# A gated trunk layer in float32 pairs: the order of the last two gate cells, the first loads, and the sums of squares

## The chip, the cores and the metric

One Trainium2 chip, one NeuronCore in use. The metric is the device time of one execution of the whole program in microseconds (us), the median of several runs. A profile of one execution gives the times of single instructions. The engines are called PE (TensorE, the matrix engine), DVE (VectorE), ACT (ScalarE), POOL (GpSimd) and SP (SyncE, which here only issues transfers).

## What is computed

One decoder layer (sequence 1024, width 1024) and a final RMSNorm. Shortened:

```python
h = rms_norm(x, norm_mix_g)
q, k, v, z_a, gk_low, cb, cc, xc, z_c, g_a, g_c = split(h @ w_in)
gk = log_sigmoid(gk_low @ w_gk2 + b_gk) / 16
o = rms_norm(gla_chunked(q, k, v, gk), gla_norm_g)        # linear attention, 4 heads, chunks of 64
y_a = (o * silu(z_a)) @ w_branch_a
y_c = ((cb * causal_dwconv(cc * xc, conv_w)) * silu(z_c)) @ w_branch_c
merged = sigmoid(g_a + b_ga) * y_a + sigmoid(g_c + b_gc) * y_c
x = x + merged @ w_out
ple_gate = sigmoid(rms_norm(x, norm_ple_g) @ w_ple_gate)
x = x + ple_gate * (p @ w_ple_proj)                        # p: (1024, 256)
return rms_norm(x, norm_final_g)
```

## The kernel before

**Products.** Every large product is made from pairs: a float32 tile is split into a rounded part `hi` (a cast on ACT) and a rest `lo = src - hi` (a subtraction on DVE), and `mm3` issues three matrix instructions for one 128x512 product: hi times hi, hi times lo, lo times hi. Large products go by a seven-product scheme for a two by two split (products 0 to 6 in place of eight). A `Cell` holds one such scheme for 256 rows or columns of the result. Product k of a cell takes twelve matrix instructions (four K-tiles times three). The running sums are in three PSUM banks X, Y and V: products 0 and 3 end in X, which is quarter (0,0); Y starts as a copy of product 0 and takes 2, 4 and 6; V takes 1 and 5. Two intermediate values are kept in SBUF: `c12` (tag u2, Y after product 2) and `c22` (tag s5, V after product 1). Quarter (0,1) is V after product 5 plus c12, quarter (1,1) is Y after product 4 plus c22, quarter (1,0) is Y after product 6. `cons(i, j, src)` consumes a finished quarter. `run_groups` lists the products of the cells; in a pair the two cells alternate product by product, in the order `PAIR` (0, 1, 2, 3, 5, 4, 6). Operands are loaded and split up to seven products ahead.

**Stages.** At the start the projection `pe` = p times w_ple_proj is computed in blocks of 128 rows (`pe_blocks`) and stored to DRAM, while x is loaded. Ten filler products (`warm`) on a cleared tile (`zero`) run before it. `scale_h` forms the mean squares of x for one half of the sequence: four squares on ACT (scaled by 1/32), added on DVE into a tile of two K-tiles, then summed over the partitions by one-column products with a vector of ones (`ms`), four blocks of 128 tokens times two K-tiles, each in full float32. From the result come r (a power on POOL), its transposes `rt` and the scaled `hq`. Then come the gates, v, the conv branch, attention woven between the gate cells, the two branch projections, the output projection (`out0` to `out3`), and last the gate cells `gt0` to `gt3`, 256 rows each, with everything that closes the layer in their consumer.

**The closing.** For each quarter of a gate cell: a sigmoid on ACT with the row scale `rg`, its product with `pe` and the addition to x on DVE, and the square of the new x on ACT with an accumulated row sum. When both halves of a row are there, `rf` = (mean square + eps) to the power -1/2 on POOL, then the multiplication with rf and the gain `gf`, and a store. For some rows (`late_cons`, `piece`) the first half is multiplied by gf in advance. The very last product (cell 3, product 6) is made in two halves of 256 columns (`last_product`), the second into another bank, Z.

**Order.** The program is recorded first (`Flow.note`), with a cost for each instruction and a latency behind it. `set_dues` works back from the end to a due time for each, and `put_in_order` steps through time, taking for the engine that is free first the ready instruction with the earliest due time; on PE the products of the cells keep their written order (`side = False`), and others (sums, transposes, attention) fall between. `hurry` moves a due time up. The result is a fixed order for each engine, SP's queue of transfers included, and each engine runs it strictly in that order. All compute instructions are recorded through one helper, so the profile shows them all at one line (L491) and they are told apart by their tiles.

Of the kernel before, what the change touches and what calls it, by code (L numbers as in the profile page):

```python
# [246 lines left out]
class Flow:  # L247
# [12 lines left out]
    def note(self, engine, op, call, args, kw):  # L260
# [15 lines left out]
        if engine == PE:  # L276
            o.cost, o.lat = n / 2400 + 0.0134, 0.22
            if op == "transpose" or args[1].dtype == F32:
                o.cost = 0.11
            elif args[1].shape[0] < P:  # L280
                o.cost = 0.42
# [10 lines left out]
        elif engine == POOL:  # L292
            o.cost = 0.1 + n * 0.001 if op == "memset" else 0.6
# [110 lines left out]
    def put_in_order(self):  # L404
# [28 lines left out]
        while len(order) < len(ops):  # L433
            best = None
            for e in range(5):
# [12 lines left out]
                best = (when, e, first[1] if pick is None else pick)  # L448
            assert best, "nothing can run"
# [49 lines left out]
START = 30.0  # L499


@with_exitstack
def kernel(
# [197 lines left out]

    ORDER, PAIR = tuple(range(7)), (0, 1, 2, 3, 5, 4, 6)

    class Cell:


        def __init__(self, name, side, src, res, cons, prods=ORDER, begin=None, s1=None, u2=None, s5=None, fresh=()):
# [3 lines left out]
            self.s1, self.seed, self.ready, self.halves = s1, None, lambda k: True, None  # L711
# [12 lines left out]
        def prep(self, k):  # L724
            if k not in self.ring:
                self.load(k)
                self.ring[k] = self.steps[k]()
# [35 lines left out]
        def run(self, k):  # L763
            if k == self.prods[0]:
                if self.begin:
                    self.begin()
                self.Y = None
# [5 lines left out]
            elif k == 1:  # L773
# [28 lines left out]
    def line_up(groups):  # L802
# [3 lines left out]
        return [(c, k) for g in groups for k in g[0].prods for c in g]  # L806

    def single(cs):
        return [[c] for c in cs]

# [175 lines left out]
    nc.vector.memset(f(zero), 0.0)  # L986
# [4 lines left out]
    for n in range(10):  # L991
        mm(warm[n % 6], zero[:, 0:P], zero, start=True, stop=True)
    nc.side = True

    with phase("prep0") as pool:
# [37 lines left out]
        def scale_h(i):  # L1033
# [30 lines left out]
        def pe_blocks(bs, c, by_kt=False):  # L1064
# [5 lines left out]
            todo = [(b, kt) for kt in range(2) for b in bs] if by_kt else [(b, kt) for b in bs for kt in range(2)]  # L1070
# [709 lines left out]
```

## Time and profile before

| | |
|---|---|
| time, median of 3 runs | 1102.06 us (1101.98 to 1102.79) |
| the profiled execution: its own time | 1102.23 us |
| its span, first to last instruction | 1100.4 us |
| PE busy | 1089.4 us, 99% of the span |
| DVE, ACT, POOL busy | 855.8, 598.2, 56.0 us |
| granted PE clock | 0.998 |

Rows of the timeline read: start in us, duration in us, engine, line, operation, output tile <- input tiles, shapes, count; in brackets the time that the engine stood idle before it, and what ended that. Matrix instructions overlap, so the distance between their starts tells more than their durations. The chain of waits follows the work that ended last back to the start. SPq is SP's queue of transfers: its rows tell when a transfer was issued, not when it landed.

### The profile page before, as it was taken

The page shows a single profiled execution, that of the slowest core. Times are in us where ns is not written, and L with a number is a line of the kernel's source. Part 1 is how long each engine was busy: PE and PEld are TensorE (multiplying, and loading weights), DVE is VectorE, ACT ScalarE, POOL GpSimd, SP SyncE. Part 2 cuts the span into 40 slices and gives each one's busy share as a digit, 9 for nine tenths or more (in the row PEclk, how much of TensorE's full clock was granted, in tenths as well). Part 3 has the DMA queues.
Part 4 walks back from the last instruction along what each step waited for, and adds up shares of the span by engine and source line. Part 5 has one row for each costly group of instructions (what it writes and reads, how often), then busy time and mean ns, then how long its engine had stood idle before and what let it go on. Part 6 is the DMA issues. An engine that isn't in the chain of part 4 may idle for free.

```text
span 1100.4 us, 15273 instructions
## 1 busy us (share of the span) xinstructions
PE 1089.4 (99%) x5050; PEld 908.3 (83%) x5050; DVE 855.8 (78%) x1386; ACT 598.2 (54%) x1107; POOL 56.0 (5%) x116
## 2 busy tenths in 40 slices
PE   9999999999999999999999999999999999999996
PEld 7888888788888888888888898888888888888885
DVE  6996477789878878748649587876999889868666
ACT  6775347866543554343333377766736445457554
POOL 0000000000000000000000022230000000002021
PEclk9999999999999999999999999999999999999999
DMA  9957463358867595222212699988595888889653
GB/s 317 327 184 246 131 210 109 117 172 252 255 221 268 177 313 180 88 66 66 87 58 65 220 307 345 323 267 293 207 308 176 301 260 291 293 311 320 238 201 114
DMA packets 152574, 238.94 MB, mean 217 GB/s; under 512 B 12976, under 2 KB 66480, under 8 KB 149424
## 3 DMA queue, kind: packets, MB, share of 16 engines
q1 hardware_dynamic: 152496, 237.98, 65.0%
q8 instruction: 39, 0.64, 0.2%
q14 instruction: 39, 0.32, 0.1%
HBM read 157.19 MB, written 80.74 MB: 216 GB/s over the span
## 4 chain that ended last, share of the span: by engine, by line
PE 96%; ACT 2%; DVE 2%; issue 0%; POOL 0%; DVEq 0%; ACTq 0%
PE vacc L491 7%; PE op L491 3%; PE pe L491 2%; PE X L491 2%; PE ga2Y L491 1%; PE ga3Y L491 1%; PE ga1Y L491 1%; PE ga0Y L491 1%; PE out1Y L491 1%; PE gc1Y L491 1%; PE out0Y L491 1%; PE gc0Y L491 1%; PE out3Y L491 1%; PE out2Y L491 1%; PE za0Y L491 1%; PE xc3Y L491 1%
## 5 line engine op out<-in xcount | busy, mean ns | idle before, releaser
L491 ACT ACTIVATE junk<-x 128x512 bf16<-128x512 f32 (+1 forms) x29 | 17.8, 615 | 12.0 <-DVE x L491 11.5
L491 ACT ACT_TABLE_LOAD x17 | 21.8, 1283 | 3.4 <-issue 2.4
L491 DVE TENSOR_TENSOR wt<-wt 128x512 f32<-128x512 f32 x32 | 21.8, 685 | 1.5 <-DMA wtd<-wt 1.3
L491 POOL TENSOR_TENSOR or<-or,mhalf 128x1 f32<-128x1 f32 x32 | 20.4, 638 | 2.7
L491 DVE SCALAR_TENSOR_TENSOR u<-t,vec,u 128x1024 f32<-128x1024 f32 x16 | 20.4, 1276 | 0.0
L491 DVE COPY_PREDICATED aT<-trim,X 128x128 f32<-128x128 int32 x32 | 9.6, 301 | 13.5 <-PE X L491 13.1
L491 POOL MEMSET t<- 128x2 f32 x8 | 0.8, 99 | 378.4 <-DVE u L491 194.8
L491 ACT ACTIVATE og<-op,or 128x256 f32<-128x256 f32 x32 | 15.1, 472 | 8.9 <-POOL or L491 6.5
L491 POOL TENSOR_SCALAR rg<-ms 128x1 f32<-128x1 f32 x8 | 4.9, 612 | 265.8 <-ACT junk L491 265.7
L491 ACT CAST aTh<-aT 128x128 fp32r<-128x128 f32 x32 | 9.5, 298 | 11.4 <-DVE aT L491 9.9
L491 PE MATMUL op<-vl,aTh 128*128 128x256 f32 x64 | 15.0, 314 | 0.0
L491 POOL TENSOR_SCALAR or<-oms 128x1 f32<-128x1 f32 x32 | 8.8, 274 | 119.1 <-ACT junk L491 119.1
L491 PE MATMUL op<-Sh,qkl 128*128 128x256 f32 x56 | 14.6, 283 | 0.0
L491 DVE TENSOR_TENSOR oT<-op,szl 128x256 f32<-128x256 f32 x32 | 13.3, 420 | 0.6 <-DMA od<-oT 0.2
L491 ACT ACTIVATE junk<-op 128x256 bf16<-128x256 f32 x32 | 12.3, 384 | 2.0 <-PE op L491 1.6
L491 DVE TENSOR_TENSOR Sl<-S,Sh 128x256 fp32r<-128x256 f32 x28 | 11.8, 420 | 1.4 <-ACT Sh L491 1.1
L491 PE MATMUL pe<-wpehi,pThi 128*128 128x512 f32 x32 | 12.7, 398 | 0.0
L491 PE MATMUL pe<-wpelo,pThi 128*128 128x512 f32 x32 | 12.6, 393 | 0.0
L491 PE MATMUL pe<-wpehi,pTlo 128*128 128x512 f32 x32 | 12.5, 391 | 0.0
L491 PEld LDWEIGHTS X<-vl,keh 128*128 128x128 f32 x56 | 10.4, 188 | 2.3
L491 PE MATMUL X<-qkl 128*128 128x128 f32 x64 | 12.3, 273 | 0.0
L491 PE MATMUL op<-ident,og 128*128 128x128 f32 x64 | 12.3, 273 | 0.0
(3240 smaller groups left out, 4160.1 us busy)
## 6 DMA issues: line engine op xcount, KB each, us to landing
wtd<-wt SPq DMA_DIRECT2D x44, 256.0 KB, 3.8
qkl<-qkd SPq DMA_DIRECT2D x32, 320.0 KB, 4.9
wt<-in_wb_dram SPq DMA_DIRECT2D x8, 1024.0 KB, 6.5
vl<-vd SPq DMA_DIRECT2D x32, 256.0 KB, 4.8
vraw<-in_wb_dram SPq DMA_DIRECT2D x28, 256.0 KB, 4.4
wgq<-wtd SPq DMA_DIRECT2D x7, 1024.0 KB, 7.3
uq<-ud SPq DMA_DIRECT2D x5, 1024.0 KB, 5.6
oq<-od SPq DMA_DIRECT2D x5, 1024.0 KB, 6.1
```

Of the source, the lines that this page charges most:

```text
L491: o.call(*[place(a) for a in o.args], **{k: place(a) for k, a in o.kw.items()})
```

## The change

1. *The last pair.* Cells gt2 and gt3 form a group of their own class (`Closing`), whose 14 products follow a written list `CLOSE`: gt2's 0, 1, 3, 2, then gt3's 0, gt2's 5, 4, gt3's 3, gt2's 6, and then gt3's 2, 1, 4, 5, 6. In these two cells the addition that completes quarter (0,1) is made into V before product 5, and the consumer reads V itself. Both rows of cell 3, and the second of cell 2 as before, go through `late_cons`. Their rf is summed on POOL instead of DVE, but for the very last row. The last row's second half is stored by a transfer issued from ACT. The copy to Z takes 256 columns instead of 512 and another bank.
2. *The start.* Eight filler products instead of ten, on a cleared 128 columns read four times over; p's first 128 columns are loaded and split first, then the weights of K-tile 0, then p's other 384 columns; the products of K-tile 0 of the first four blocks run hi-hi for all blocks, then lo-hi, then hi-lo.
3. *The sums of squares.* The two K-tiles of the sum of squares are added on DVE (128x512), and the one-column products are four for each half instead of eight.
4. *Durations.* The recorded cost of a full-float32 product that is not a transpose is 0.22 instead of 0.11, that of a POOL operation 0.35 + 0.25 n instead of 0.6; a transfer issued from ACT has one. Before 35 us and after 1060 us of the planned time, DVE and ACT may leave a ready instruction for one due earlier that will be ready within 0.6 or 0.3.

The diff, cut:

```diff
-        if engine == PE:
+        if engine == ACT and op == "dma_start":
+            o.cost, o.lat = 0.1, 3.0
+        elif engine == PE:
             o.cost, o.lat = n / 2400 + 0.0134, 0.22
             if op == "transpose" or args[1].dtype == F32:
-                o.cost = 0.11
+                o.cost = 0.11 if op == "transpose" else 0.22
...
-            o.cost = 0.1 + n * 0.001 if op == "memset" else 0.6
+            o.cost = 0.1 + n * 0.001 if op == "memset" else 0.35 + 0.25 * n
...
                 best = (when, e, first[1] if pick is None else pick)
+                reach, margin = (NEAR, 0.5) if when > NEAR_END else (SOON, 1.0) if when < BEGUN else (0.0, 0.0)
+                if pick is not None and e in (DVE, ACT) and reach:
+                    soon = [(ops[n].due, n, w) for n, w in found
+                            if when < w < when + min(reach, ops[pick].cost) and ops[n].due < ops[pick].due - margin]
+                    if soon:
+                        best = (min(soon)[2], e, min(soon)[1])
...
+WARM = 8
+NEAR, NEAR_END = 0.3, 1060.0
+SOON, BEGUN = 0.6, 35.0
...
+    CLOSE = (0, 1, 3, 2, 10, 5, 4, 13, 6, 12, 11, 14, 15, 16)
...
         def last_product(self):
-            other = psm.tile([P, 512], F32, tag=f"m{3 * (1 - self.set)}", name=f"{self.name}Z")
-            nc.scalar.copy(other, self.Y)
+            other = psm.tile([P, 512], F32, tag=f"m{3 * self.set}", name=f"{self.name}Z")
+            nc.hurry = -2.5
+            nc.scalar.copy(other[:, 256:], self.Y[:, 256:])
+            nc.hurry = 0.0
...
                 self.c22 = self.taken("s5", self.V)
+                if self.closing and self.c12 is not None:
+                    tt(self.V, self.V, self.c12, op=ALU.add)
             elif k == 2:
                 self.product(2, self.Y, False)
-                self.c12 = self.taken("u2", self.Y)
+                if self.closing and self.c22 is not None:
+                    tt(self.V, self.c22, self.Y, op=ALU.add)
+                else:
+                    self.c12 = self.taken("u2", self.Y)
...
+            elif k == 5 and self.closing:
+                self.product(5, self.V, False)
+                self.cons(0, 1, self.V)
...
+            if isinstance(g, Closing):
+                todo += [(g[k // 10], k % 10) for k in CLOSE]
...
-    nc.vector.memset(f(zero), 0.0)
+    nc.vector.memset(f(zero[:, 0:P]), 0.0)
...
-    for n in range(10):
-        mm(warm[n % 6], zero[:, 0:P], zero, start=True, stop=True)
+    for n in range(WARM):
+        mm(warm[n % 6], zero[:, 0:P], zero[:, None, 0:P].to_broadcast([P, 4, P]), start=True, stop=True)
...
-        for kt in range(2):
-            load(pr_[:, kt, halves[0]], pT[:, kt, halves[0]])
-            load(wr_[:, kt, halves[0]], wpe[:, kt, halves[0]])
+        first = [(pr_, pT, 0, slice(0, P)), (wr_, wpe, 0, halves[0]), (pr_, pT, 0, slice(P, 512)),
+                 (wr_, wpe, 1, halves[0]), (pr_, pT, 1, halves[0])]
+        for t, src, kt, cs in first:
+            nc.hurry = 8.0 if cs.stop > P else 12.0
+            load(t[:, kt, cs], src[:, kt, cs])
...
+            tt(acc[:, 0, :], acc[:, 0, :], acc[:, 1, :], op=ALU.add)
             sums = pso.tile([P, 4, P], F32, tag="o", name=f"ms{i}", bufs=2)
             for s in range(4):
-                for kt in range(2):
-                    mm(sums[:, s, 0:1], acc[:, kt, s * P:(s + 1) * P], ones, start=kt == 0, stop=kt == 1)
+                mm(sums[:, s, 0:1], acc[:, 0, s * P:(s + 1) * P], ones, start=True, stop=True)
...
+            if by_kt:
+                nc.side = False
+                for p_, w_ in ((pth, wph), (ptl, wph), (pth, wpl)):
+                    for b in bs:
+                        mm(acc[b], p_[:, 0, rows(b)], w_[:, 0, halves[c]], start=w_ is wph and p_ is pth, stop=False)
+                nc.side = True
+                todo = todo[len(bs):]
...
-                    nc.vector.tensor_scalar(r, m, sums[i][:, 0:1], None, op0=ALU.add)
+                    (nc.vector if last else nc.gpsimd).tensor_scalar(r, m, sums[i][:, 0:1], None, op0=ALU.add)
                     nc.gpsimd.tensor_tensor(r, r, mhalf, op=ALU.pow)
...
+                    if last:
+                        part = xt[i][:, 512:]
+                        act(part, part, AF.Copy, scale=r[:, 0:1])
+                        nc.scalar.dma_start(out[rows(2 * p + i), 512:], part)
+                        part = xt[i][:, 0:256]
+                        nc.vector.tensor_scalar(part, part, r[:, 0:1], None, op0=ALU.mult)
+                        stt(xc, xc, r[:, 0:1], gf[:, cs], op0=ALU.mult, op1=ALU.mult)
+                        store(out[rows(2 * p + i), 0:512], xt[i][:, 0:512])
+                        return
+                    ready = slice(512, D) if a == 0 else slice(0, 512)
+                    act(xt[i][:, ready], xt[i][:, ready], AF.Copy, scale=r[:, 0:1])
+                    store(out[rows(2 * p + i), ready], xt[i][:, ready])
                     stt(xc, xc, r[:, 0:1], gf[:, cs], op0=ALU.mult, op1=ALU.mult)
...
-                    if i == 1 and p >= 2:
+                    if p == 3 or p == 2 and i == 1:
                         return late_cons(i, j, src)
...
-            run_groups(pairs(gts))
+            run_groups(pairs(gts[:2]) + [Closing(gts[2:])])
```

More of the change, by code (lines that the diff above doesn't have):

```diff
@@ L710, in __init__ @@
             self.get = {"u2": u2, "s5": s5}
-            self.s1, self.seed, self.ready, self.halves = s1, None, lambda k: True, None
+            self.s1, self.seed, self.ready, self.halves, self.closing = s1, None, lambda k: True, None, False
             self.raw, self.ring = [None] * 4, {}
@@ L1098 @@
         nc.hurry = 8.0
[L1099 to L1101 removed]
+        for t, _, kt, cs in first:
+            hi, lo = (pth, ptl) if t is pr_ else (wph, wpl)
+            nc.hurry = 8.0 if cs.stop > P else 12.0
+            split(hi[:, kt, cs], lo[:, kt, cs], t[:, kt, cs])
         nc.hurry = 0.0
@@ L1643, in piece @@
                 def piece(i, cs, src, n, done):
-                    w = cs.stop - cs.start
-                    a = cs.start
+                    w, a, last = cs.stop - cs.start, cs.start, p == 3 and i == 1
                     if a % 512 == 0:
@@ L1656, in piece @@
                         tt(xc, xc, gf[:, cs], op=ALU.mult)
-                        pre = gp.tile([P, 1], F32, tag="pre", name=f"pre{p}_{i}_{n}", bufs=4)
+                    if not done:
+                        pre = gp.tile([P, 1], F32, tag="pre", name=f"pre{p}_{i}_{n}", bufs=8)
                         nc.vector.tensor_scalar(pre, m, EPS if n == 0 else sums[i][:, 0:1], None, op0=ALU.add)
@@ L1704, in cons @@
                         store(out[rows(2 * p + i), :], xt[i])
-                cell.cons = cons
+                cell.cons, cell.closing = cons, p >= 2
                 if p == 3:
```

29 lines of the change are left out of this document (15 added, 14 removed).

## The prediction

> **What bounds the kernel now.** I read the busy shares first, then the chain that ended last, then what TensorE (PE) waited for, then busy time by stretch.
>
> ```profile
> span 1100.4 us, 15273 instructions
> PE 1089.4 (99%) x5050; PEld 908.3 (83%) x5050; DVE 855.8 (78%) x1386; ACT 598.2 (54%) x1107; POOL 56.0 (5%) x116
> PE 96%; ACT 2%; DVE 2%; issue 0%; POOL 0%; DVEq 0%; ACTq 0%
> PE warm L491 <- DVE zero L491: 1.4, 1, 1.4
> PE za2Y L491 <- ACT za2u L491: 0.2, 1, 0.2
> 45.00:1040.00 995.00, 994.81 (x4618) 829.89 (x4617) 777.05 (x1267) 537.18 (x997) 41.55 (x93) 1.00 0.65 216
> 1040.00:1091.00 51.00, 50.96 (x236) 42.23 (x234) 38.02 (x57) 27.14 (x58) 10.66 (x12) 1.00 0.46 160
> 1091.00:1100.40 9.40, 0.03 (x1) 0.00 (x0) 5.54 (x16) 2.90 (x9) 1.48 (x2) 0.71 0.30 112
> ```
>
> In the stretch rows the first pair is length and PE's busy time. PE is never free between the first microseconds and 1091: the chain is PE for 96%, and its waits after the start add up to 0.2. So the time is (when useful products begin) + (PE work) + (what follows the last product, 9.4). Nothing in the middle can be won; there the new durations can only cost. The change touches all three terms.
>
> **Term 1, the start.** Ten filler products become eight, over a cleared tile of 128 columns instead of 512; p's first 128 columns are loaded ahead of the weights, the rest of that block behind them; the first K-tile's twelve products run part by part instead of row block by row block.
>
> ```profile
> 1.44 3.78 PE L491 MATMUL warm<-zero 128*128 128x512 f32 x8 [1.44 <-DVE zero L491]
> 5.02 1.05 PE L491 MATMUL warm<-zero 128*128 128x512 f32 x2
> 5.87 0.52 PE L491 MATMUL pe<-wpehi,pThi 128*128 128x512 f32 x1
> 6.23 0.40 PE L491 MATMUL pe<-wpelo,pThi 128*128 128x512 f32 x1
> 8.74 0.39 PE L491 MATMUL pe<-wpehi,pThi 128*128 128x512 f32 x1
> 9.19 0.43 PE L491 MATMUL pe<-wpehi,pTlo 128*128 128x512 f32 x1
> 3.60 0.62 ACT L491 CAST wpehi<-wperaw 128x512 fp32r<-128x512 f32 x1 [1.60 <-DMA wperaw<-in_wpe_dram]
> 4.39 0.62 ACT L491 CAST pThi<-pTraw 128x512 fp32r<-128x512 f32 x1 [0.17 <-DMA pTraw<-in_pT_dram]
> 5.54 0.62 ACT L491 CAST wpehi<-wperaw 128x512 fp32r<-128x512 f32 x1 [0.53 <-DMA wperaw<-in_wpe_dram]
> 7.72 0.62 ACT L491 CAST pThi<-pTraw 128x512 fp32r<-128x512 f32 x1 [1.56 <-DMA pTraw<-in_pT_dram]
> 8.37 0.69 DVE L491 TENSOR_TENSOR pTlo<-pTraw,pThi 128x512 fp32r<-128x512 f32 x1 [1.49 <-ACT pThi L491]
> ```
>
> Filler products start 0.43 apart (the ninth at 5.02, the first useful one two later at 5.87); useful ones run 0.23 apart from 6.23 on. After: the weights are the second transfer behind a quarter-size one, so they land between 3.60 and 4.39, say 3.9; their cast (0.62) ends about 4.55; the filler, begun some 0.3 earlier behind the smaller clear, ends about 4.7. The first useful product comes at 4.7 instead of 5.87, the second waits for the cast of p's other 384 columns (about 5.1), two or three more run at 0.43 until the clock rises near 6, the rest at 0.23: the twelve end about 8.2 instead of 8.74, 0.55 earlier. That gain lasts only if the second K-tile of p is there. In this run it was the limit: its cast could begin only at 7.72, and the third product of that K-tile was pushed to 9.19 by its low part (8.37 + 0.69). After, it is the fifth transfer instead of the fourth, with the same 1 MB up to its end. The landings before it were 0.8 and 1.15 apart, this one 2.2, so part of the 7.72 looks like a delay of this execution. Gain: 0 if it lands as here, 0.55 if a microsecond sooner, -0.4 if its later issue moves it; I take **0.3**.
>
> The filler is there for the clock, and the step from 0.43 to 0.23 about 4.5 after PE's first product is in the rows. The Trainium skill (TensorE: Matmul & The Clock Gate, Part 1: The HAM clock gate) says that the clock rises after about 3.4 us of sustained activity in a window that runs freely, not after a count of products. By that rule eight cold products still suffice; by its free window the step can fall later, which is a rival below.
>
> **Term 2, the sums of squares.** Per half of x, 8 one-column products become 4, and one 128x512 add on DVE comes in front.
>
> ```profile
> 18.99 1.85 PE L491 MATMUL ms<-ones,sq 128*128 128x1 f32 x16
> 20.70 0.49 PE L491 MATMUL pe<-wpehi,pThi 128*128 128x512 f32 x1
> 42.66 1.84 PE L491 MATMUL ms<-ones,sq 128*128 128x1 f32 x16
> 44.36 0.49 PE L491 MATMUL ga0pX<-h3lo,ga0phi 128*128 128x512 f32 x1
> 15.10 1.07 ACT L491 ACTIVATE sr<-hq 128x1024 f32<-128x1024 f32 x1 [0.42 <-DMA hq<-in_xT_dram]
> 15.34 0.68 DVE L491 TENSOR_TENSOR pTlo<-pTraw,pThi 128x512 fp32r<-128x512 f32 x1
> 17.55 1.22 DVE L491 TENSOR_TENSOR sq<-sq 128x1024 f32<-128x1024 f32 x1
> 29.09 1.22 DVE L491 TENSOR_TENSOR h0lo<-hq,h0hi 128x1024 fp32r<-128x1024 f32 x1
> 30.35 2.72 PE ga0pX L491 x12
> ```
>
> The 8 products are 16 records and hold PE for 20.70 - 18.99 = 1.71 and 44.36 - 42.66 = 1.70. Half gone is 0.85 each, 1.7 in all, straight off PE's path. The new add (as 15.34: 0.68) must be hidden: in the built order the sums stand five products later (5 x 0.23 = 1.1), so they are due at 18.99 + 1.1 - 0.3 = 19.8. The DVE now has both low parts of p's second half, two wide adds (1.2 each) and the narrow one to do from about 15.4 (the third square no longer stands behind a cast): 1.3 + 2.4 + 0.6 ends at 19.7. That just fits; 0.2 is lost if the start gains its full 0.55. The second half has six products more in front and a DVE add of the same size: it fits likewise. Behind the sums, h0's scaling moves some 0.6 later, but the four scalings and both h0lo now follow without a copy between them: last h0lo done about 29.9, needed about 1.6 (seven products) after ga0pX begins at 30.35 - 1.2, at 30.7. Covered by 0.8; without the cover it would cost the difference. I take **1.6** (1.4 to 1.7).
>
> **Term 3, the last pair.** Before, gate cells 2 and 3 alternate; after, cell 2 finishes six products before the end and cell 3 closes alone, its (0,1) quarter from PSUM with u and s5 added beforehand.
>
> ```profile
> 1087.47 0.39 PE L491 MATMUL gt2Y<-wg6hi,gt2lo 128*128 128x512 f32 x1
> 1087.90 0.39 PE L491 MATMUL gt3Y<-wg6hi,gt3hi 128*128 128x256 f32 x1
> 1091.47 0.63 ACT L491 ACTIVATE junk<-x 128x512 bf16<-128x512 f32 x1 [0.28 <-DVE x L491]
> 1092.10 0.43 ACT L491 ACTIVATE gt3Z<-gt3Z,rg 128x256 f32<-128x256 f32 x1
> 1094.20 0.21 DVE L491 TENSOR_SCALAR rf<-msl,pre 128x1 f32<-128x1 f32 x1
> 1093.77 1.48 POOL L491 TENSOR_TENSOR rf<-rf,mhalf 128x1 f32<-128x1 f32 x2 [7.84 <-DVE rf L491]
> 1096.19 0.35 DVE L491 TENSOR_SCALAR x<-x,rf 128x256 f32<-128x256 f32 x1
> 1095.24 1.97 SPq L491 DMA_DIRECT2D out_dram<-x  x4
> L491 POOL TENSOR_SCALAR rf<-ms x6: 301/1186/2603, 1044.1 to 1083.7; 128x1 f32<-128x1 f32 x6
> ```
>
> PE first: 1087.90 - 1087.47 = 0.43 where 0.23 is the rhythm: the last product waited 0.2 for DVE's add on gt3Y. After, a whole product lies between that add and the last product: **0.2** off. Then the chain behind the last product (1091.0): the last sigmoid (gt3Z) could be taken at once, but ACT was still squaring cell 2's row (1091.47) and came to it at 1092.10, 1.0 late. After, ACT still has x_3_0's square and the first quarter's sigmoid in front: I place it at 1091.25, 0.85 sooner. DVE's gain multiply of x_3_1 holds the next step up by some 0.3, so the last rf, ready at 1094.41, comes about 0.55 sooner; POOL then has one power to do instead of two (1.48 for both), and DVE two operations of 256 columns behind it instead of four scalings of cell 2 and 3. Last DVE operation 1096.54, after about 1095.45: 1.1 sooner. From there the stores: four of 256 KB, as before; the two of x_3_0 leave about 0.8 before the last pair, one of which goes out from ACT's queue beside SP's. Sharing the same transfers costs some of the gain. No run here shows a store issued from ACT; by the SP row (1.97 for four) its issue is worth at most 0.5 either way. Against it: x_3_0's rf is now made on POOL, and DVE's order has its scaling ahead of the last rf. POOL's first step took 0.30 to 2.60 in six cases; above about 1.3 it delays the end, at worst by 0.8. I take **1.0** (0.3 to 1.6).
>
> The rule behind that row speaks against this edit: the Trainium skill (GPSIMD Engine Reference, 1. Specifications) says POOL shares its SBUF interfaces with VectorE, with contention when a DVE operation has two SBUF inputs. By it the step lasts while DVE's tensor-tensor run does, and the term would be near 0.3.
>
> **Sum.** 0.3 + 1.6 + 0.2 + 1.0 = 3.1. Truer durations move ACT, DVE and DMA orders in the v and attention stretches; PE waited 0.2 there in all, so their worth is 0, at worst -0.5. The profiled execution took 1102.23 (span 1100.4 and 1.8 around it); the runs' median is 1102.06, 0.2 below. 1102.06 - 3.1 = **1099.0**.
>
> **Rivals.** *The closing is not shorter*: POOL's step stretches, or the four stores end as late because they are one stream. For it: 2.60 in the row. Against: DVE goes idle when it has nothing left, and the last pair of stores is fewer bytes behind the last scaling. 1099.0 + 0.9 = 1099.9. Chance 0.15.
>
> *The clock rises late*: fewer filler products and a gap of 0.4 behind the first useful one. If the twelve all run 0.43 apart they end at 4.7 + 5.2 = 9.9, 1.1 behind before; with the 0.3 lost, 1099.0 + 1.4 = 1100.4. Against: PE is busy over the same stretch up to 6. Chance 0.09. (The skill's free window allows this in some executions and not in others.)
>
> *The sums wait*: the longer DVE chain shows, in both halves, for the 0.68 of the add: 1099.0 + 1.3 = 1100.3. Chance 0.07.
>
> *Slower*: in the last pair, adds that PE waits for now stand on DVE behind closing work: gt2's V add behind x_2_0's, which waits for its load, and gt3's V add behind cell 2's last scaling, which waits for POOL.
>
> ```profile
> 1052.34 0.39 PE L491 MATMUL gt2X<-wg0hi,gt2hi 128*128 128x512 f32 x1
> 1060.77 1.51 SPq L491 DMA_DIRECT2D x<-x2d  x1
> DMA to landing us min/median/max: 2.6/4.9/7.1
> ```
>
> Gt2's V is needed after five products, 1052.34 + 13.6 = 1065.9. Issued as late as before and landing in 7.1, the load is there at 1067.9; with two DVE operations PE waits 3.3; a POOL step of 2.60 behind gt3's V would add about 2.2. 1099.0 + 5.5 = 1104.5. It decides from an issue later than about 1058; the new order puts this load ahead of three stores that it stood behind, near 1057, and gt3's V has about a microsecond in hand. Chance 0.06.
>
> **Numbers.** My forecast has 0.63. The terms' bounds give 1098.0 to 1101.3 if all fall together; 1097.8 to 1101.0 leaves out the slower rival and the corners. About 0.2% (2.2 us) is what a measurement of this kernel can tell from no change: faster means below 1099.9. Of the forecast nearly all, of the first rival half, of the others little: faster 0.71, same 0.23, slower 0.06.
>
> **What would show it.** In the profile after: useful products from about 4.7 and the second K-tile's at or before 8.7; ms with 8 records a half, 0.85 long, no idle in front; no PE gap over 0.1 between 1040 and the end; gt3Z's sigmoid within 0.4 of the last product; span minus the last product about 8.3 instead of 9.4. It is wrong if PE shows new waits in the last pair, if the twelve first products run 0.43 apart, or if the closing stays above 9.

## The result and the profile after

| | before | after |
|---|---|---|
| median | 1102.42 us (10 runs, 1101.98 to 1103.38) | 1099.40 us (10 runs, 1098.29 to 1100.92) |
| ratio, 95% interval | | 0.9972 [0.9964, 0.998] |
| the profiled execution: its own time | 1102.23 us | 1100.92 us |
| its span | 1100.4 us | 1098.9 us |

The kernel became 3.0 us faster (forecast: 1099.0, that is 3.1 faster). The profiled execution after was the slowest of its ten, 1.5 above their median. So its trace shows what can go wrong as well as what went right, and part of what follows is to tell the two apart. First the page, the waits of PE and the busy time by stretch, as before. (The helper's line is L499 in the changed kernel, and L491 or L493 where part of the change is left out.)

```profile
span 1098.9 us, 15245 instructions
PE 1088.8 (99%) x5032; PEld 905.9 (82%) x5032; DVE 856.8 (78%) x1389; ACT 599.9 (55%) x1109; POOL 56.7 (5%) x117
```

```profile
PE pe L499 <- ACT pThi L499: 0.5, 1, 0.5
PE op L499 <- DVE oT L499: 0.2, 1, 0.2
```

```profile
45.00:1040.00 995.00, 994.46 (x4618) 829.07 (x4617) 778.58 (x1270) 536.76 (x996) 43.59 (x93) 1.00 0.65 217
1040.00:1090.00 50.00, 50.00 (x230) 41.75 (x229) 39.37 (x61) 27.79 (x58) 9.10 (x12) 1.00 0.45 163
1090.00:1098.90 8.90, 1.00 (x9) 0.80 (x7) 4.46 (x13) 3.49 (x10) 1.93 (x3) 0.83 0.31 118
```

PE has two new waits, one at the start for p's cast (0.5) and one in attention (oT). Between 45 and 1040 it is busy for 994.46 of 995.00, where it was 994.81 before. In the stretch with the last pair, 1040 to 1090, it is busy throughout, 50.00 of 50.00.

The start, from the timeline:

```profile
4.72 2.46 PE L499 MATMUL pe<-wpehi,pThi 128*128 128x512 f32 x4
7.02 1.09 PE L499 MATMUL pe<-wpehi,pTlo 128*128 128x512 f32 x4
7.94 1.09 PE L499 MATMUL pe<-wpelo,pThi 128*128 128x512 f32 x4
8.89 0.62 ACT L499 CAST pThi<-pTraw 128x512 fp32r<-128x512 f32 x1 [2.17 <-DMA pTraw<-in_pT_dram]
9.56 0.50 PE L499 MATMUL pe<-wpehi,pThi 128*128 128x512 f32 x1 [0.53 <-ACT pThi L499]
```

Useful products begin at 4.72, as forecast (4.7), and the twelve of the first K-tile end near 9.0. But p's second K-tile was cast only at 8.89 (before: 7.72), and PE came to its products at 9.56 (before: 8.74).

The sums of squares and h0 behind them:

```profile
21.29 0.99 PE L499 MATMUL ms<-ones,sq 128*128 128x1 f32 x8
22.14 0.48 PE L499 MATMUL pe<-wpehi,pTlo 128*128 128x512 f32 x1
28.73 2.43 DVE L499 TENSOR_TENSOR h0lo<-hq,h0hi 128x1024 fp32r<-128x1024 f32 x2
30.47 0.39 PE L499 MATMUL ga0pX<-h0hi,ga0phi 128*128 128x512 f32 x1
30.70 0.39 PE L499 MATMUL ga0pX<-h0lo,ga0phi 128*128 128x512 f32 x1
45.20 0.95 PE L499 MATMUL ms<-ones,sq 128*128 128x1 f32 x8
46.01 0.49 PE L499 MATMUL ga1pX<-h3hi,ga1plo 128*128 128x512 f32 x1
```

A half now holds PE for 22.14 - 21.29 = 0.85 and 46.01 - 45.20 = 0.81 instead of 1.71 and 1.70: 1.75 less together, with no idle time in front. The products with h0's low part follow without a hole.

The closing:

```profile
1090.73 0.28 PE L499 MATMUL gt3Z<-wg6hi,gt3lo 128*128 128x256 f32 x1
1091.04 0.45 ACT L499 ACTIVATE gt3Z<-gt3Z,rg 128x256 f32<-128x256 f32 x1
1091.20 0.70 POOL L499 TENSOR_SCALAR rf<-msl,pre 128x1 f32<-128x1 f32 x1 [9.94 <-ACT junk L499]
1093.26 0.21 DVE L499 TENSOR_SCALAR rf<-msl,pre 128x1 f32<-128x1 f32 x1
1093.37 1.98 SPq L499 DMA_DIRECT2D out_dram<-x  x3
1093.55 0.66 POOL L499 TENSOR_TENSOR rf<-rf,mhalf 128x1 f32<-128x1 f32 x1 [0.99 <-DVE rf L499]
1094.52 0.48 DVE L499 SCALAR_TENSOR_TENSOR x<-x,rf,gfin 128x256 f32<-128x256 f32 x1
1095.00 0.39 ACTq L499 DMA_DIRECT2D out_dram<-x  x1
```

The last sigmoid starts right behind the last product (1091.04; before 1092.10), the last rf 0.94 sooner, the last DVE operation ends at 1095.00 instead of 1096.54.

So in this execution the parts add up to the 1.5 us between the spans like this. The last product starts at 1090.73, where before it started at 1090.75: at the start about 1.2 was lost, the sums gave 1.7, attention took 0.8, the last pair gave 0.3, some 0.15 went in the output projection, and nothing is left. All 1.5 lie behind the last product.

### The profile page after: what moved, and what is told of

It is laid out like the page before. It is cut to its first block, busy times and chain, and to the rows that moved or that the text cites. A ratio compares the mean times of both kernels' runs of the same rounds, so it can differ in the third digit from the quotient of the medians.

```text
span 1098.9 us, 15245 instructions
## 1 busy us (share of the span) xinstructions
PE 1088.8 (99%) x5032; PEld 905.9 (82%) x5032; DVE 856.8 (78%) x1389; ACT 599.9 (55%) x1109; POOL 56.7 (5%) x117
## 4 chain that ended last, share of the span: by engine, by line
PE 94%; DMA 3%; DVE 1%; ACT 1%; issue 0%; SPq 0%; POOL 0%; POOLq 0%; DVEq 0%; ACTq 0%
PE vacc L499 7%; PE pe L499 2%; PE op L499 2%; DMA od<-oT 1%; PE X L499 1%; PE out1Y L499 1%; PE gc0Y L499 1%; PE out0Y L499 1%; PE out2Y L499 1%; PE out3Y L499 1%; PE gc1Y L499 1%; PE za0Y L499 1%; PE xc3Y L499 1%; PE xc2Y L499 1%; PE xc1Y L499 1%; PE cb0Y L499 1%
## 5 line engine op out<-in xcount | busy, mean ns | idle before, releaser
L499 DVE TENSOR_TENSOR wt<-wt 128x512 f32<-128x512 f32 x32 | 21.8, 687 | 1.9 <-DMA wtd<-wt 1.7
L499 ACT ACTIVATE junk<-x 128x512 bf16<-128x512 f32 (+1 forms) x29 | 17.8, 615 | 9.7 <-DVE x L499 7.9
L499 POOL TENSOR_TENSOR or<-or,mhalf 128x1 f32<-128x1 f32 x32 | 21.4, 669 | 2.7
L499 ACT ACTIVATE og<-op,or 128x256 f32<-128x256 f32 x32 | 15.1, 471 | 10.7 <-POOL or L499 7.0
L499 DVE SCALAR_TENSOR_TENSOR u<-t,vec,u 128x1024 f32<-128x1024 f32 x16 | 20.5, 1280 | 0.0
L499 POOL MEMSET t<- 128x2 f32 x8 | 0.8, 100 | 378.4 <-DVE u L499 194.8
L499 DVE TENSOR_TENSOR oT<-op,szl 128x256 f32<-128x256 f32 x32 | 13.5, 422 | 7.9 <-DMA od<-oT 5.2
L499 POOL TENSOR_SCALAR rg<-ms 128x1 f32<-128x1 f32 x8 | 4.4, 553 | 269.4 <-ACT junk L499 269.3
L499 DVE COPY_PREDICATED aT<-trim,X 128x128 f32<-128x128 int32 x32 | 9.6, 300 | 7.9 <-PE X L499 7.2
L499 POOL TENSOR_SCALAR or<-oms 128x1 f32<-128x1 f32 x32 | 9.5, 297 | 114.9 <-ACT junk L499 114.9
L499 PE MATMUL op<-vl,aTh 128*128 128x256 f32 x64 | 15.1, 317 | 0.2 <-DVE oT L499 0.2
L499 PE MATMUL op<-Sh,qkl 128*128 128x256 f32 x56 | 14.6, 283 | 0.0
L499 PE MATMUL pe<-wpehi,pThi 128*128 128x512 f32 x32 | 13.4, 431 | 0.6 <-ACT pThi L499 0.5
L499 ACT ACTIVATE junk<-op 128x256 bf16<-128x256 f32 x32 | 12.3, 384 | 2.3 <-PE op L499 2.0
L499 ACT CAST aTh<-aT 128x128 fp32r<-128x128 f32 x32 | 9.5, 298 | 7.0 <-DVE aT L499 6.6
L499 DVE TENSOR_TENSOR Sl<-S,Sh 128x256 fp32r<-128x256 f32 x28 | 11.8, 420 | 1.2 <-ACT Sh L499 1.0
L499 PE MATMUL op<-ident,og 128*128 128x128 f32 x64 | 12.3, 273 | 0.1
L499 PEld LDWEIGHTS X<-vl,keh 128*128 128x128 f32 x56 | 10.5, 188 | 2.3
L499 PE MATMUL X<-qkl 128*128 128x128 f32 x64 | 12.3, 273 | 0.0
L499 PE MATMUL pe<-wpehi,pTlo 128*128 128x512 f32 x32 | 12.2, 397 | 0.0
L499 PE MATMUL pe<-wpelo,pThi 128*128 128x512 f32 x32 | 12.1, 394 | 0.0
```

The source lines that it names most:

```text
L499: o.call(*[place(a) for a in o.args], **{k: place(a) for k, a in o.kw.items()})
```

## The experiments

Twelve runs followed: ten other kernels, and the changed one twice more. Each ratio is to the kernel before, measured beside it (medians 1102.36 to 1102.56). The intervals are about 1 us wide on either side, so a difference of a few tenths is read from the rows, which are those of one profile each.

The table gives what the timelines show: the form of the start, the time of the first product of the second block of columns (the 25th useful one), the order of the attention stage, the stretch from the first product of ga0V to the first of yc0X (the attention stretch), what oT on DVE waited there for its stores, and the time from the start of the last product to the end of the span. Spans are given to 0.1, so the last column is good to 0.05.

| profile | start | 25th product | attention order | ga0V to yc0X | oT waits for od | last product to end |
|---|---|---|---|---|---|---|
| before | old | 11.50 | old | 158.70 | 0.2 | 9.65 |
| after | new | 12.68 | new | 159.47 | 5.2 | 8.17 |
| after_again | new | 11.26 | new | 159.81 | 5.1 | 8.14 |
| after_third | new | 11.55 | new | 158.63 | 2.2 | 8.07 |
| no_dur | new | 10.95 | old | 158.68 | none | 8.16 |
| sums_only | old | 12.14 | old | 158.66 | none | 9.71 |
| close_only | old | 11.87 | old | 158.66 | none | 8.16 |
| ms_cost | new | 11.64 | old | 158.66 | 0.5 | 8.13 |
| no_start | old | 12.20 | new | 158.71 | 2.4 | 8.09 |
| sp_store | new | 12.17 | new | 158.69 | 1.9 | 8.43 |
| rf_dve | new | 13.37 | new | 158.63 | 2.4 | 8.39 |
| ms_warm10 | new, ten fillers | 11.11 | old | 158.73 | 0.5 | 8.09 |
| ms_warm_parts | new, ten fillers | 11.66 | old | 158.72 | none | 8.12 |
| dur_only | old | 11.32 | new | 158.77 | 1.9 | 9.90 |

**The changed kernel again.** No edit; a second profile, and later a third.

> The changed kernel once more, for a second profile. In the first one p's second K-tile was cast only at 8.89 and PE reached the second K-tile's products at 9.56, about 1 us behind the kernel before, and two gaps of PE (523 and 489 ns between starts near 687 us) lay in the attention stretch. Theory 1 (the late transfer was that execution's): the cast comes before 8.3, the second K-tile's products begin by 8.7, and this execution takes 1099.0 to 1099.6. Theory 2 (the new load order delays p's second K-tile every time): again 8.7 or later for the cast, and products from 9.4. On the attention stretch: if its loss belongs to the new order, the two gaps near 687 are there again within 0.2 us of their size; if it belongs to how the transfers fell in one execution, they are gone or elsewhere.

1098.84 us (7 runs, 1098.56 to 1101.12), ratio 0.9971 [0.9961, 0.9982]; the profiled execution took 1099.72.

```profile
6.68 0.62 ACT L499 CAST pThi<-pTraw 128x512 fp32r<-128x512 f32 x1
8.54 0.39 PE L499 MATMUL pe<-wpehi,pThi 128*128 128x512 f32 x1
617.62 0.39 PE L499 MATMUL ga0V<-h1hi,ga0hi 128*128 128x512 f32 x1
777.43 0.39 PE L499 MATMUL yc0X<-u0hi,yc0hi 128*128 128x512 f32 x1
```

The cast of p's second K-tile came at 6.68, 2.2 us sooner than in the first profile of the same kernel, and the products followed at 8.54: the late transfer was that execution's, theory 1. The attention stretch was long again (159.81), with its two gaps between product starts at the same places (0.77 and 0.49), and with that the time is 0.1 over theory 1's.

> The changed kernel a third time, beside the two versions below on one chip. The stretch from ga0V to yc0 took 158.63 to 158.71 us in all five profiles of the old attention order and in three of the five of the new one, and 159.46 and 159.81 in the other two. Theory 1 (the new order is exposed to when transfers land, and is longer in some executions): either 158.6 to 158.8 or over 159.3. Theory 2 (a matter of the chip): like the other kernels of this call with the new order. Time 1098.8 to 1099.6.

1100.05 us (11 runs, 1098.48 to 1103.12), ratio 0.9976 [0.9967, 0.9985], profiled at 1100.58. The attention stretch was short this time (158.63): theory 1. Its lost time lies elsewhere, in the convolution branch, where the change does nothing:

```profile
416.39 0.72 ACT L499 ACTIVATE wt<-wt,vec 128x512 f32<-128x512 f32 x1 [4.14 <-DMA wtd<-wt]
```

```profile
PE xc1Y L499 <- ACT xc1u L499: 1.6, 1, 1.6
```

ACT waited 4.14 for a store of wt to land, the copy of xc1u stood behind it, and PE for that one: 1.94 between two product starts, 419.05 and 420.99. At the same place there are 0.74 in no_dur and 0.68 in no_start, and the usual 0.23 in the other profiles. The median of these runs lies just above the 1098.8 to 1099.6 that were expected.

**The truer durations undone, and alone.** Item 4 has two parts, the durations and the rule for what DVE and ACT may leave for later. (The line of the rule that begins with `soon =` reads `for w, n in found` in the kernel that ran.) Both are undone in the change:

```diff
-                o.cost = 0.11 if op == "transpose" else 0.22
+                o.cost = 0.11
...
-            o.cost = 0.1 + n * 0.001 if op == "memset" else 0.35 + 0.25 * n
+            o.cost = 0.1 + n * 0.001 if op == "memset" else 0.6
...
-                reach, margin = (NEAR, 0.5) if when > NEAR_END else (SOON, 1.0) if when < BEGUN else (0.0, 0.0)
```

> The change without the truer durations and without the new rule for what DVE and ACT leave for a later instruction (a transfer issued from ACT keeps its cost). Attention then runs in the order of the kernel before. Theory 1 (the new durations cost 0.77 us in the attention stretch, seen in the first two profiles between 620 and 742 us): 0.5 to 0.8 us faster than the change, about 1098.7, ratio to the kernel before 0.9965. Theory 2 (what the new durations bring at the start and in the closing is worth as much or more): as the change or slower, 1099.4 to 1100.2.

1099.84 us (11 runs, 1099.03 to 1101.55), ratio 0.9977 [0.9968, 0.9986]. Attention took 158.68, as theory 1 wanted, but the kernel was not faster (after_again, on the same chip, has 1098.84): theory 2 by its time, and the rows say by which means.

```profile
28.72 0.39 PE L493 MATMUL ga0pX<-h0hi,ga0phi 128*128 128x512 f32 x1
29.53 0.50 PE L493 MATMUL ga0pX<-h0lo,ga0phi 128*128 128x512 f32 x1 [0.42 <-DVE h0lo L493]
30.79 0.40 PE L493 MATMUL ga0pX<-h0hi,ga0phi 128*128 128x512 f32 x1
31.32 0.50 PE L493 MATMUL ga0pX<-h0lo,ga0phi 128*128 128x512 f32 x1
27.65 0.69 DVE L493 COPY pe<-pe 128x512 f32<-128x512 f32 x1
28.25 1.22 DVE L493 TENSOR_TENSOR h0lo<-hq,h0hi 128x1024 fp32r<-128x1024 f32 x1
29.39 0.74 DVE L493 SCALAR_TENSOR_TENSOR hq<-hq,vec,rt 128x512 f32<-128x512 f32 x1
30.04 1.22 DVE L493 TENSOR_TENSOR h0lo<-hq,h0hi 128x1024 fp32r<-128x1024 f32 x1
```

Where the rhythm is 0.23, there are 0.81 and 0.53: PE waits twice for h0's low part, 0.9 in all and another 0.2 in the starts right behind. Without item 4 the order on DVE puts a copy of pe ahead of the first h0lo and a scaling between the two, which stand together in the change (28.73, x2). The cover that the prediction counted on (0.8) is gone. So item 4 saves about 1.1 here and costs 0 to 1.1 in attention. Which part of it moves h0's work was not taken apart.

The same hunks alone, on the kernel before:

> The kernel before with the truer durations and the new rule alone. Theory 1 (they win only where the sums of squares were shortened: there PE waited 1.1 us for h0's low part without them; alone they move the attention order, worth 0 to 1.1 us against): 0 to 1.1 us slower than before, 1102.3 to 1103.5. Theory 2 (they also improve the start or the closing by themselves): 0.3 to 0.8 faster.

1102.78 us (11 runs, 1101.79 to 1105.12), ratio 1.0003 [0.9994, 1.0012]: no difference. Theory 1, at its lower end: attention took 158.77 in this profile. In the last pair the old order of products lost its wait here too: from gt2X's first product to the last one it was 38.1, as in the change, where the kernel before has 38.4. But 0.2 was lost again behind the last product (9.90).

**Which duration moves attention.**

```diff
-                o.cost = 0.11 if op == "transpose" else 0.22
+                o.cost = 0.22 if n == 1 else 0.11
```

> The change, but the longer recorded cost (0.22) goes to the one-column products alone; every other product in full float32 keeps 0.11. The order of the start and of the closing is then that of the change, the order of the attention stretch that of the kernel before. Theory 1 (the attention stretch from ga0V to yc0 takes 158.7 us in the old order and 159.5 to 159.8 in the new one, because stores of oT land late there): 0.8 to 1.1 us faster than the change, about 1098.0, ratio to the kernel before 0.9960. Theory 2 (the attention stretch varies by execution, and the two profiles of the change happened on long ones): the same as the change, 1098.8 to 1099.4, with 158.7 to 159.8 in the profile.

1099.26 us (5 runs, 1098.87 to 1099.43), ratio 0.9968 [0.9956, 0.9981]. The attention stretch is 158.66, in the order of the kernel before instruction by instruction, and h0 has its cover. So it is the longer cost of the products in full float32 that are more than one column wide that moves attention, and h0's cover does not need it. The time does not stand apart from the change's in so few runs; the expected 1098.0 was too low, since the change itself is long in attention only in some executions. What the two orders differ in is how exposed they are. The waits around oT in the attention stretch, first in the change's first profile, then in ms_cost:

```profile
DVE oT L499 <- DMA od<-oT: 5.2, 4, 2.6
ACT og L499 <- DVE oT L499: 3.6, 4, 1.7
```

```profile
DVE oT L499 <- DMA od<-oT: 0.5, 1, 0.5
```

In all seven profiles of the new order oT waits 1.9 to 5.2 us for its stores to land; in all seven of the old one 0 to 0.5. In its seven profiles PE loses nothing from waits of up to 2.4 in all, and 0.8 and 1.1 where they add up to over 5. Why they were over 5 in the first two profiles and not in the five later ones stays open. In the first profile of the change this is one of the places:

```profile
685.40 0.42 DVE L499 TENSOR_TENSOR oT<-op,szl 128x256 f32<-128x256 f32 x1 [2.62 <-DMA od<-oT]
685.92 0.47 ACT L499 ACTIVATE og<-op,or 128x256 f32<-128x256 f32 x1 [0.92 <-DVE oT L499]
688.95 0.47 PE L499 MATMUL op<-vl,aTh 128*128 128x256 f32 x2 [0.22 <-DVE oT L499]
```

oT waits 2.62 for a buffer whose store is still under way, og waits 0.92 for oT, and PE's next product starts 0.52 instead of 0.23 behind the one before, at 686.45. At 688.95 PE waits again, for oT itself.

**The sums of squares alone.**

```diff
+            tt(acc[:, 0, :], acc[:, 0, :], acc[:, 1, :], op=ALU.add)
...
-                for kt in range(2):
-                    mm(sums[:, s, 0:1], acc[:, kt, s * P:(s + 1) * P], ones, start=kt == 0, stop=kt == 1)
+                mm(sums[:, s, 0:1], acc[:, 0, s * P:(s + 1) * P], ones, start=True, stop=True)
```

> The kernel before with the sums of squares alone changed (both K-tiles added on DVE, four products a half instead of eight). Theory 1 (1.70 us of products a half become 0.85, and the new add is hidden): 1.6 to 1.7 us faster, ratio 0.9985, and no idle time of PE ahead of ms. Theory 2 (the add stands in PE's way): 0.3 to 1.0 us faster, with PE waiting 0.3 to 0.7 ahead of ms.

1101.32 us (11 runs, 1100.75 to 1101.64), ratio 0.9988 [0.9979, 0.9997], so 1.0 us faster, with an interval of 0.3 to 2.3.

```profile
PEld ga0pX L491 <- DVE h0lo L491: 0.7, 2, 0.6
```

Nothing is idle ahead of ms, so theory 2's place was wrong, but its size was nearer: part of the gain comes back as a wait for h0's low part, behind the sums, not ahead of them. On PE it is about 0.4 (0.53 instead of 0.23 between two starts at 31.3, and 0.1 behind), so the rows leave some 1.3 of 1.75. The time alone can't tell that from 1.0 or 1.7. (This profile's start was 0.6 later than before's.)

**The last pair alone.** All of item 1 of the change on the kernel before, with the recorded cost of a transfer issued from ACT; of it:

```diff
+    CLOSE = (0, 1, 3, 2, 10, 5, 4, 13, 6, 12, 11, 14, 15, 16)
...
+            elif k == 5 and self.closing:
+                self.product(5, self.V, False)
+                self.cons(0, 1, self.V)
...
-            run_groups(pairs(gts))
+            run_groups(pairs(gts[:2]) + [Closing(gts[2:])])
```

> The kernel before with the last pair alone changed (order of the products, sums of quarter (0,1) ahead, both rows of cell 3 finished in halves, the first part of the last store from ACT). Theory 1 (the two profiles: 9.4 us behind the last product became 7.9, and 0.2 of waiting before it is gone): 1.7 us faster, ratio 0.9985, with the last product's start to the span's end 7.9 to 8.1. Theory 2 (the closing was forecast at 1.0, and the rest of the 1.5 came from the new durations): 1.0 to 1.3 faster, with 8.3 to 8.6 behind the last product.

1100.89 us (11 runs, 1100.04 to 1101.48), ratio 0.9986 [0.9977, 0.9994], so 1.5 faster, between the two theories.

```profile
1090.74 0.28 PE L493 MATMUL gt3Z<-wg6hi,gt3lo 128*128 128x256 f32 x1
1091.06 0.45 ACT L493 ACTIVATE gt3Z<-gt3Z,rg 128x256 f32<-128x256 f32 x1
```

The span is 1098.9: 8.16 behind the last product's start instead of 9.65. That is nearer theory 1 (7.9 to 8.1) than theory 2 (8.3 to 8.6), and the same as in the change: beside the new last pair, the new durations add nothing to the closing.

**The last store from SP.**

```diff
-                        nc.scalar.dma_start(out[rows(2 * p + i), 512:], part)
+                        store(out[rows(2 * p + i), 512:], part)
```

> The change with the last row's second half stored by SP like the other three instead of by ACT. Theory 1 (the issue from ACT takes one of four issues, about 0.5 us, off SP's queue): 0.3 to 0.5 us slower than the change, with the last transfer issued 0.4 later. Theory 2 (the transfers share the same engines and end together): within 0.1 behind the last product, about 8.1 as in the change.

1099.19 us (6 runs, 1098.51 to 1100.35), ratio 0.9969 [0.9957, 0.998].

```profile
1089.27 0.28 PE L499 MATMUL gt3Z<-wg6hi,gt3lo 128*128 128x256 f32 x1
1091.88 2.84 SPq L499 DMA_DIRECT2D out_dram<-x  x4
```

SP's four issues end at 1091.88 + 2.84 = 1094.72, 5.45 behind the start of the last product. With ACT's help the last one ends at 1095.39, 4.66 behind. The end is 8.43 behind instead of 8.07 to 8.17: 0.8 of issue is worth some 0.3 in this profile, at the lower end of theory 1's 0.3 to 0.5. The time (1099.19) does not show it. The Trainium skill (Trainium Kernel Development and Optimization, Key Constraints) says that transfers issued from several engines share the same sixteen DMA engines, and that this saves issue time only; the trace agrees in that the gain is smaller than the issue saved.

**rf on DVE.**

```diff
-                    (nc.vector if last else nc.gpsimd).tensor_scalar(r, m, sums[i][:, 0:1], None, op0=ALU.add)
+                    nc.vector.tensor_scalar(r, m, sums[i][:, 0:1], None, op0=ALU.add)
```

> The change with the sums for rf of cell 2's second row and cell 3's first row on DVE again instead of POOL. POOL's step took 0.70 us in the closing, DVE's 0.15 to 0.21. Theory 1 (off the path: x_3_0's step only decides when its stores leave): the same, 8.0 to 8.2 us behind the last product. Theory 2 (DVE's queue becomes longer, which is what the step on POOL spares): 0.2 to 0.4 slower. Theory 3 (POOL's 0.70 delays x_3_0's stores and with them the end): 0.2 to 0.5 faster.

1099.74 us (6 runs, 1098.36 to 1100.87), ratio 0.9971 [0.9959, 0.9983]. The end lies 8.39 behind the last product, 0.2 to 0.3 later: theory 2 by this profile, which the time does not show. The last rf comes 2.81 behind the last product (1093.22 and 1090.41), 2.53 in the change: DVE's queue is the path there, and POOL's 0.70 lies beside it. This profile also shows the rival of the late clock:

```profile
4.88 0.80 PE L499 MATMUL pe<-wpehi,pThi 128*128 128x512 f32 x1
6.02 1.65 PE L499 MATMUL pe<-wpehi,pThi 128*128 128x512 f32 x3 [0.35 <-ACT pThi L499]
7.47 1.91 PE L499 MATMUL pe<-wpehi,pTlo 128*128 128x512 f32 x4
9.18 1.61 PE L499 MATMUL pe<-wpelo,pThi 128*128 128x512 f32 x4
10.63 0.40 PE L499 MATMUL pe<-wpehi,pThi 128*128 128x512 f32 x1
```

The starts are 0.43 apart (7.47 to 9.18 is four of them) until past 10. The twelve end at 10.6, where the rival of the prediction said 9.9, though p's second K-tile was cast at 7.71.

**The start undone.** Ten wide fillers, the old loads, row block by row block.

> The change with the kernel before's start (ten wide filler products, p's and the weights' K-tiles loaded in turn, row block by row block). In the profiles so far the first block of products (24) ends between 11.5 and 12.1 us after the start in the old form and between 11.0 and 12.7 in the new. Theory 1 (the new start is worth about 0.3 in the median, with a wider spread): 0.2 to 0.5 us slower than the change, 1099.2 to 1099.6. Theory 2 (it is worth nothing, since p's second K-tile decides in both): within 0.2 of the change. Theory 3 (it costs): 0.3 or more faster.

1099.6 us (6 runs, 1098.57 to 1100.67), ratio 0.9972 [0.9961, 0.9984]. It is not to be told from the change, and it lies between theories 1 and 2. (This profile also lost time in the convolution branch, the 0.68 above.) The table says the same: the 25th product comes at 11.32 to 12.20 with the old start (median of five 11.87), at 10.95 to 13.37 with the new one and eight fillers (median of seven 11.64). The new start gains 0.2 in the middle and spreads over 2.4 us instead of 0.9.

**Ten fillers, and the second K-tile part by part.** ms_cost with ten fillers on the small tile; and that with the second K-tile's products of the first four blocks part by part, p's low part last.

```diff
-WARM = 8
+WARM = 10
```

> As ms_cost (0.22 for the one-column products alone), with ten filler products instead of eight, on the small cleared tile. In the six profiles of the new start the clock rose 4.7 to 6.0 us after PE's first product, and 9.4 in the one where PE stood longest between the first useful product and the second (twelve products 0.43 apart, as in the rival of the late clock). Theory 1 (the hole behind the first useful product delays the clock, and two more filler products fill it): no gap over 0.6 between starts before the clock rises, the clock up by 6.2 after PE's start, the 24 first products done by 11.0 to 12.2, a time of 1098.6 to 1099.1 with no run above 1100. Theory 2 (the clock's window runs by itself, the hole has no part in it): the spread stays, 1098.5 to 1100.5, median as the change or 0.3 slower.

1098.88 us (5 runs, 1098.44 to 1099.22), ratio 0.9967 [0.9955, 0.998].

```profile
5.39 1.29 PE L499 MATMUL pe<-wpehi,pThi 128*128 128x512 f32 x4
6.51 1.08 PE L499 MATMUL pe<-wpehi,pTlo 128*128 128x512 f32 x4
8.34 0.39 PE L499 MATMUL pe<-wpehi,pThi 128*128 128x512 f32 x1
```

Useful products begin at 5.39, 0.7 later than in the first profile of the change, and without a hole behind the first; the clock was up at 6.05, and the second K-tile's products began at 8.34, earlier than in six of the seven profiles with eight fillers. This fits theory 1 but does not show it: with the next one there are two profiles.

```diff
+                for p_, w_ in ((pth, wph), (pth, wpl)):
+                    for b in bs:
+                        mm(acc[b], p_[:, 1, rows(b)], w_[:, 1, halves[c]], start=False, stop=False)
```

> As ms_warm10, and the second K-tile's twelve products of the first four blocks also run part by part: high by high for all four, then with the weights' low parts, and p's low part last. In the profiles PE waited 0.0 to 0.5 ahead of the third product of that K-tile for p's low part. Theory 1 (that low part is on the path): 0.2 to 0.4 faster than ms_warm10, no wait for pTlo there. Theory 2 (the arrival of p's second K-tile itself is the limit, or what follows waits for the four copies that now come together): within 0.1, or slower by up to 0.4.

1098.68 us (5 runs, 1098.66 to 1099.58), ratio 0.9968 [0.9955, 0.998]: as ms_warm10, theory 2. The clock rose at 7.08 here, which set the start: 6.0 us after PE's first product, without a hole, and 5.0 in ms_warm10. Both lie within what the profiles with eight fillers show (4.7 to 6.2, but for rf_dve), so the two more fillers are not seen to steady the clock.

On the chip of the last two the change had 1100.05. The intervals of the ratios overlap, so the medians alone don't rank them. All fifteen runs of the three ms_ kernels are at or below 1099.58, while twelve of the change's 28 are above. They keep what the change wins and are steadier; that they are faster in the median is likely, by about half a microsecond, and not shown.

## Why the prediction was right, and where not

*The sum.* 3.1 was forecast and 3.0 measured (1102.42 - 1099.40), inside the range. That they are so close is in part luck. The terms, as the rows below give them, come to about 0 + 1.75 + 0.3 + 1.5 = 3.6, and the closing alone was 0.5 above its forecast. Against them stand waits in the middle of the kernel that the forecast put at 0, at worst 0.5: in the three profiles of the change 0.8 and 1.1 in attention, and 1.7 in the convolution branch. No profile shows an execution at the median, so where the missing 0.6 went in it is not shown.

*Sums of squares, 1.6.* The mechanism and the size hold: 1.75 from the rows, with no wait in front in the change's first profile. In no_start, ms_cost and ms_warm10 the products did wait 0.2 for the new add in the first half (in no_start it ended at 20.44 and they began at 20.58, 0.45 behind the product ahead instead of 0.23), the loss that the prediction had named. The step that decides is the cover for h0's low part, which the prediction read from the built order, 0.8 in hand. The runs show that it comes from item 4: without it PE waits 1.1 (no_dur), and the sums alone keep some 1.3 of their 1.75 (sums_only).

*The closing, 1.0.* Under-sized: 1.5 by the spans of after and of close_only. The sigmoid came at 1091.04 (1091.25 forecast), and the last rf was held up by the gain multiply of x_3_1 for 0.1 only, where 0.3 had been taken off: 0.94 sooner instead of 0.55. POOL's step took 0.70, below the 1.3 from which it would have delayed the end. The transfer from ACT is worth some 0.3 of it (sp_store), POOL's sum 0.2 to 0.3 (rf_dve), each by one profile. By the rule of the shared SBUF interfaces in the Trainium skill (GPSIMD Engine Reference, 1. Specifications) the prediction had worked out a term near 0.3; these runs don't show that here.

*PE's wait in the last pair, 0.2.* From gt2X's first product to the last one it was 1090.75 - 1052.34 = 38.4 before and 38.1 after, 0.3 less. The new order of products is not the only way to that: dur_only has 38.1 with the old one. No new wait appeared, so the slower rival did not come about: the adds on V were in time. (By the list `CLOSE`, five products follow gt2's last one, not six; nothing in the sum hangs on it.)

*The start, 0.3.* Nearly nothing, 0.2 in the middle of the profiles and nothing that the times tell apart, and the spread is larger than the bounds taken (-0.4 to +0.55): against the profile of before, one lost 1.2 and one 1.9 (25th product). The step that failed is that the useful products' early begin counts. They do begin earlier, at 4.72 to 5.13 instead of 5.48 to 5.87, but the rest hangs on two things that vary by more: when p's second K-tile lands (cast at 6.38 to 8.38 in the old start and 6.68 to 8.89 in the new), and when the clock rises. One row was misread: the product at 9.19 was not pushed by p's low part, for it starts 0.23 behind the one ahead (8.96). In the profile of before p's second K-tile came just in time, and PE never waited for it. The rival of the late clock was counted at 0.09 and came in one of seven profiles.

*The truer durations, 0, at worst -0.5.* The net was taken as near 0, but it is made of two parts that were not seen: 1.1 for h0 at the start, and against it an attention order that is exposed to its own stores, at a cost of 0 in five of seven profiles and of 0.8 and 1.1 in two. "PE waited 0.2 there in all" was true of the old order only, and said nothing on how much room a new one leaves.

## What to carry to other kernels

Where a planner's order hides a step, ask which recorded durations made it do so, and expect that the gain of an edit is not its own: by the rows the sums of squares were worth 1.75 with the new durations and some 1.3 without. A truer duration written for a whole kind of instruction also moves those that did not need it; give it to the instructions that needed it, and look at the waits of the engines that are not the bound (oT's 5 us), since they show exposure before PE does. A start of ten microseconds varies by more than its edits are worth, so it is judged over several profiles, not from one.

## What the runs showed of the hardware

The clock's rise is the surprise. In thirteen of fourteen profiles products came 0.23 apart from 3.5 to 6.2 us after PE's first product on; in rf_dve only after 9.4, with PE idle for about 0.7 us between the first useful product and the second (4.88 and 6.02, less the 0.43 that a product takes before the rise). The Trainium skill (TensorE: Matmul & The Clock Gate, Part 1: The HAM clock gate) gives a free-running window of 3.4 us and a spread of half a microsecond for the step. The free window fits these times if a window with such a hole does not count as busy (3.5 to 6.2 is within one to two windows, 9.4 is in the third); the spread here was far larger. Against it, in the first profile of the change PE stood idle for 0.45 at the same place (4.72 and 5.60), and the clock still rose at 7.0. So if the hole is the cause, 0.45 was short enough and 0.7 was not. No run took the hole alone away, so the cause stays open.

Transfers of one kernel land differently from execution to execution: the same 256 KB of p, issued at the same place, were cast at 6.68, 7.17 and 8.89 in the three profiles of the change. A store's landing stopped ACT for 4.14 us and PE for 1.6 in one profile of a stage that the change does not touch.
